# A fused LoRA matmul: the small stores ahead of one chunk's big store are cut differently and all go through GpSimd's queue

## The chip, the cores and the metric

The kernel runs on one core of a Trainium2 chip. A core has a matrix engine (TensorE, in the profile PE for matmuls and PEld for weight loads), VectorE (DVE), ScalarE (ACT), GpSimd (POOL), a queue processor (SyncE, SP) and 16 DMA engines that all queues share. Transfers issued by SP or ACT go through hardware queues; those issued by GpSimd go through a software queue, q0 in the profile. The metric is device time in microseconds of one execution.

## The reference

`x` has 16 x 2048 rows of 256 float32 numbers; `W` is 256 x 256, `lora_A` 256 x 16, `lora_B` 16 x 256, `lora_E` 16 numbers, `scale` 1.0.

```python
y = x_flat @ W
lora_out = x_flat @ lora_A
lora_out = lora_out * lora_E
lora_out = lora_out @ lora_B
y = y + scale * lora_out
```

The output is as large as `x`: 32768 rows of 1 KB, 33.55 MB in and 33.55 MB out.

## The kernel before

The low-rank part is folded into the weight once: `weff = W + A diag(E) B`, in bfloat16, so that one product per row is left.

The 32768 rows are cut into 4 chunks. A chunk is 128 partitions x 64 rows: partition p holds 64 neighbouring rows of x, 64 KB. A chunk lives in a home in SBUF, of which there are three; chunk 3 uses the home of chunk 0 again, so that its loads must wait for chunk 0's stores. The result of a row overwrites the row in its home, and is stored from there.

A chunk is worked on in 16 groups of 4 rows per partition, 64 groups in all. For each group GpSimd casts the rows to bfloat16 (line 193), TensorE transposes them (line 244), VectorE copies the transposed rows out of PSUM (line 228), TensorE multiplies (line 255), and ScalarE copies the result home (line 209). The five engines pass groups on by semaphores.

The order of the loads and stores on SP's queue is written by hand: `ORDER` at line 18. Each entry is a load ("L") or a store ("S"), a chunk and a range of its 64 rows. `sync_program` goes through it. A store waits for `s_done`, the count of finished stretches of rows; a load of chunk 3 waits for the overlapping stores of chunk 0.

Two special rules stand around the edit. First, at group (chunk 2, row 16), called `HELD`, GpSimd waits for the store of chunk 0, rows 0 to 40, to land (lines 185 to 190). Second, the first two rows of chunk 1 (`SHARED`) do not go with the big store of chunk 1, which stores rows 2 to 64. They are stored in shares of partitions: 0 to 5 and 5 to 126 by GpSimd when it gets to `HELD`, and 126 to 128 by SP just ahead of the big store (line 159). All of them wait for `s_shared`, which ScalarE raises after the first group of chunk 1 (lines 210 and 211). A transfer over many partitions is divided among the DMA engines by partition.

The program ends when SP has seen the shares land (line 162) and, in `wait_for_stores`, when `stored_rest` has counted the stores that nothing else waits for.

Of the kernel before, what the change touches and what calls it, by code (L numbers as in the profile page):

```python
# [7 lines left out]
P = 128  # L8
# [5 lines left out]
ROWS = 64  # L14
# [3 lines left out]
ORDER = [  # L18
    ("A",),
    ("L", 0, 0, 8),  # L20
    ("L", 0, 8, 24),
    ("L", 0, 24, 40),
    ("L", 0, 40, 64),
    ("L", 1, 0, 32),
    ("L", 1, 32, 64),
    ("L", 2, 0, 16),
# [2 lines left out]
    ("S", 0, 40, 64),  # L29
    ("L", 3, 0, 32),  # L30
    ("L", 3, 32, 64),
    ("S", 1, 2, 64),
    ("S", 2, 0, 64),
    ("S", 3, 0, 64),
]

SHARED = (1, 0, 2)
SHARES = ((0, 5), (5, 126))

HELD = (2, 16)  # L40
HOLDERS = (("S", 0, 0, 40),)
# [3 lines left out]
CG = 4  # L45
# [9 lines left out]
def kernel(  # L55
# [20 lines left out]
    y_chunks = out_flat.rearrange("(c p b) m -> c p b m", p=P, b=ROWS)  # L76
# [18 lines left out]
    waited = {  # L95
        op
        for op in ORDER
        if op[0] == "S" and (op in HOLDERS or op[1] < N_CHUNKS - N_HOMES)
    }
    stored = {op: sem(f"stored_{op[1]}_{op[2]}") for op in ORDER if op in waited}  # L100
    s_shared = sem("shared_done")
    shared_stored = sem("shared_stored")
    stored_rest = nc.alloc_semaphore("stored_rest")
    n_rest = 1 + sum(op[0] == "S" and op not in waited for op in ORDER)
    ends = sorted((c * ROWS + e) // CG - 1 for kind, c, s, e in (op for op in ORDER if op[0] == "S"))
    s_ident = sem("ident_made")
    s_pe_set_up = sem("pe_set_up")
# [8 lines left out]
    def home(c):  # L116
        return homes[c % N_HOMES]

    sync, gpsimd, scalar, vector, tensor = nc.sync, nc.gpsimd, nc.scalar, nc.vector, nc.tensor
# [20 lines left out]
    def sync_program():  # L140
        for n, op in enumerate(ORDER):
            if op[0] == "A":
                a = lora_A.rearrange("(q t) r -> q t r", t=KT)
                ins = sync.dma_start(out=a_sb[:], in_=a).then_inc(set_up_loaded["a"], 16)
                opening.append(ins.ins.name)
                continue
            kind, c, s, e = op
            at_home = home(c)[:, s:e, :]
            if kind == "L":
                for st in stored:  # L150
                    if st[1] == c - N_HOMES and st[2] < e and s < st[3]:
                        sync.wait_ge(stored[st], 16)
                ins = sync.dma_start(out=at_home, in_=x_chunks[c, :, s:e, :]).then_inc(loaded[op], 16)  # L153
                if n == 1:
                    opening.append(ins.ins.name)
            else:
                if c == SHARED[0]:
                    sync.wait_ge(s_shared, 1)
                    share(sync, SHARES[-1][1], P, stored_rest)
                sync.wait_ge(s_done, ends.index((c * ROWS + e) // CG - 1) + 1)  # L160
                sync.dma_start(out=y_chunks[c, :, s:e, :], in_=at_home).then_inc(stored.get(op, stored_rest), 16)
        sync.wait_ge(shared_stored, 16 * len(SHARES))

    def share(engine, first, last, landed):
        c, s, e = SHARED
        engine.dma_start(out=y_chunks[c, first:last, s:e, :], in_=home(c)[first:last, s:e, :]).then_inc(landed, 16)  # L166

    def gpsimd_program():
        gpsimd.memset(ident[:], 0.0).then_inc(s_ident, 1)  # L169
        gpsimd.wait_ge(s_ident, 1)  # L170
        gpsimd.affine_select(  # L171
            out=ident[:],
            in_=ident[:],
            compare_op=ALU.not_equal,
            fill=1.0,
            base=0,
            pattern=[[-1, P]],
            channel_multiplier=1,
        ).then_inc(s_ident, 1)
        for g in range(N_GROUPS):  # L180
            c, b = g // GPC, g % GPC * CG
            for op, landed in loaded.items():
                if op[1:3] == (c, b):
                    gpsimd.wait_ge(landed, 16)
            if (c, b) == HELD:
                gpsimd.wait_ge(s_shared, 1)
                for s, e in SHARES:
                    share(gpsimd, s, e, shared_stored)
                for op in HOLDERS:
                    gpsimd.wait_ge(stored[op], 16)  # L190
            if g >= NS:
                gpsimd.wait_ge(s_turned, g - NS + 1)
            gpsimd.tensor_copy(out=stage[g % NS][:], in_=home(c)[:, b:b + CG, :]).then_inc(s_stage[g % UNROLL], 1)  # L193

        gpsimd.wait_ge(s_turned, N_GROUPS - NS + 1)
        gpsimd.drain().then_inc(s_stage[N_GROUPS % UNROLL], 1)

    def scalar_program():
        for name, to, of in (
            ("w", w_sb, W.rearrange("(q t) m -> q t m", t=KT)),  # L200
            ("b", b_sb, lora_B),
            ("e", e_sb, lora_E[:, None]),
        ):
            ins = scalar.dma_start(out=to[:], in_=of).then_inc(set_up_loaded[name], 16)
            opening.append(ins.ins.name)
        for g in range(N_GROUPS):
            c, b = g // GPC, g % GPC * CG
            scalar.wait_ge(s_y, g + 1)
            scalar.copy(out=home(c)[:, b:b + CG, :], in_=psum_y[g % NY][:]).then_inc(s_free[(g + NY) % UNROLL], 1)  # L209
            if (c, b) == SHARED[:2]:  # L210
                scalar.drain().then_inc(s_shared, 1)
            if g in ends:
                scalar.drain().then_inc(s_done, 1)  # L213
# [76 lines left out]
    with tc.tile_critical(no_gpsimd_drain=True):  # L290
        sync_program()
        gpsimd_program()
        scalar_program()
        vector_program()
        tensor_program()
# [35 lines left out]
```

## Time and profile before

| | |
|---|---|
| median of 10 runs | 162.17 us (161.56 to 162.98) |
| the profiled execution's own time | 161.5 us |
| its span, first to last instruction | 160.2 us |
| HBM read and written | 33.85 MB and 33.55 MB, 421 GB/s over the span |
| busy: PE, DVE, ACT, POOL | 58%, 28%, 41%, 42% of the span |
| packets of SP's queue (q1) | 97.6% of the time of 16 DMA engines |
| packets of GpSimd's queue (q0) | 112 packets, 0.26 MB, 0.4% |

Everything in the profile is from one execution. A DMA engine's time is counted by packets: the share of a queue is the time its packets took, over 16 engines and the span. In views that cut a stretch into slices, a packet is counted in the slice in which it starts, so that a share can be above 1 in a short slice. TensorE's clock (PEclk) is what the throttle granted. A DMA's "us to landing" is from its issue to the last of its 16 completion signals.

### The profile page before, as it was taken

The numbers are of one execution on the slowest core, as the hardware profiler recorded it, in microseconds if no ns is written. First come the engines' busy times: TensorE is split into PE (matmuls) and PEld (weight loads), VectorE is DVE, ScalarE is ACT, GpSimd is POOL, SyncE is SP. The second block draws the span as 40 slices with busy tenths as digits, with TensorE's granted clock in tenths as the row PEclk, the third lists the DMA queues.
The fourth block names the chain that finished last, engine by engine and source line by source line (L and its number), as shares of the span: only waits on it lengthen the run. The fifth ranks groups of instructions, "written<-read, shape, count | busy, mean of one in ns | idle before, by whom it ended". The sixth has DMA issues, their size and how long they took to land.

```text
span 160.2 us, 2030 instructions
## 1 busy us (share of the span) xinstructions
PE 93.1 (58%) x782; PEld 82.0 (51%) x782; DVE 45.4 (28%) x66; ACT 66.1 (41%) x65; POOL 67.9 (42%) x72
## 2 busy tenths in 40 slices
PE   2959969959999990000999999999920000000000
PEld 1439959859999990000789999999910000000000
DVE  0245535525555550000145555555500000000000
ACT  3025775747777772000257777777740000000000
POOL 1537838387777732002567777787200000000000
PEclk9999999999999999555589999999985555555555
DMA  6999999999999997979999999989997998998993
GB/s 260 403 430 462 417 458 401 475 434 393 417 434 528 454 393 327 496 344 448 442 448 428 409 434 466 495 349 444 491 450 344 491 442 376 491 442 376 491 426 131
DMA packets 2631, 67.43 MB, mean 421 GB/s; under 512 B 496, under 2 KB 512, under 8 KB 708
## 3 DMA queue, kind: packets, MB, share of 16 engines
q1 hardware_dynamic: 2308, 66.87, 97.6%
q10 hardware_dynamic: 208, 0.28, 0.5%
q0 software_dynamic: 112, 0.26, 0.4%
q14 instruction: 3, 0.02, 0.0%
HBM read 33.85 MB, written 33.55 MB: 421 GB/s over the span
## 4 chain that ended last, share of the span: by engine, by line
DMA 43%; PE 26%; POOL 1%; ACT 1%; SPq 0%; issue 0%; ACTq 0%
DMA out_dram<-home 30%; PE psum_y L255 17%; DMA home<-in_x_dram 12%; PE psum_xt L244 9%; POOL stage L193 1%; ACT home L209 1%; SPq L153 0%; ACTq L213 0%; SPq L326 0%; SPq L290 0%
## 5 line engine op out<-in xcount | busy, mean ns | idle before, releaser
L209 ACT COPY home<-psum_y 128x1024 f32<-128x1024 f32 x64 | 64.8, 1012 | 49.9 <-PE psum_y L255 49.9
L193 POOL CAST stage<-home 128x1024 bf16<-128x1024 f32 x64 | 66.1, 1040 | 38.7 <-PE psum_xt L244 15.0
L255 PE MATMUL psum_y<-weff,xt 128*128 128x256 bf16 x512 | 68.1, 277 | 0.0
L228 DVE COPY xt<-psum_xt 128x1024 bf16<-128x1024 bf16 x64 | 44.3, 692 | 62.7 <-PE psum_xt L244 62.7
L255 PEld LDWEIGHTS psum_y<-weff,xt 128*128 128x128 bf16 x512 | 50.9, 100 | 5.8
L244 PE MATMUL psum_xt<-ident,stage 128*128 128x128 f32 x260 | 40.3, 278 | 21.0 <-POOL stage L193 20.5
L244 PEld LDWEIGHTS psum_xt<-ident,stage 128*128 128x128 f32 x260 | 31.0, 144 | 23.6 <-issue 22.2
L268 PE MATMUL psum_y<-ident 128*128 128x512 f32 x4 | 3.7, 1081 | 2.9 <-POOL ident L171 2.9
L268 PEld LDWEIGHTS psum_y<-ident 128*128 128x128 f32 x4 | 1.2, 326 | 3.9 <-POOL ident L171 2.9
L166 POOL DMA_DIRECT2D out_dram<-home x2 | 1.2, 596 | 4.6 <-DMA home<-in_x_dram 4.6
L218 DVE TENSOR_SCALAR ate<-psum_y,e_sb 16x256 f32<-16x256 f32 x1 | 0.5, 471 | 6.9 <-PE psum_y L271 6.9
L209 ACT ACT_TABLE_LOAD x1 | 1.3, 1283 | 2.1 <-SPq L290 2.1
L277 PE MATMUL psum_y<-b_sb,ate 16*128 16x256 f32 x4 | 1.1, 393 | 0.0
L169 POOL MEMSET ident<- 128x128 f32 x1 | 0.2, 204 | 1.7 <-SPq L290 1.7
L271 PEld LDWEIGHTS psum_y<-ident,a_sb 128*16 128x16 f32 x2 | 0.2, 114 | 1.2 <-issue 1.2
L232 DVE TENSOR_TENSOR weff<-w_sb,psum_y 128x512 bf16<-128x512 f32 x1 | 0.7, 689 | 0.5 <-PE psum_y L277 0.5
L277 PEld LDWEIGHTS psum_y<-b_sb,ate 16*128 16x128 f32 x4 | 0.7, 184 | 0.3 <-issue 0.2
L171 POOL TENSOR_SCALAR_AFFINE_SELECT ident<-ident 128x128 f32<-128x128 f32 x1 | 0.3, 287 | 0.2 <-POOL ident L169 0.2
L271 PE MATMUL psum_y<-ident,a_sb 128*16 128x128 f32 x2 | 0.4, 272 | 0.0
L312 POOL MEMSET const-float32-0.0<- 128x1 f32 x1 | 0.1, 98 | 0.2 <-issue 0.2
L312 POOL MEMSET const-bfloat16-1.0<- 128x1 bf16 x1 | 0.1, 101 | 0.0
L312 POOL MEMSET const-uint8-127<- 128x1 uint8 x1 | 0.1, 101 | 0.0
(1 smaller groups left out, 0.1 us busy)
## 6 DMA issues: line engine op xcount, KB each, us to landing
home<-in_x_dram SPq DMA_DIRECT2D x4, 4096.0 KB, 24.6
out_dram<-home SPq DMA_DIRECT2D x1, 7936.0 KB
home<-in_x_dram SPq DMA_DIRECT2D x3, 2048.0 KB, 13.1
home<-in_x_dram SPq DMA_DIRECT2D x1, 6144.0 KB, 57.3
out_dram<-home SPq DMA_DIRECT2D x1, 5120.0 KB, 48.4
home<-in_x_dram SPq DMA_DIRECT2D x1, 3072.0 KB, 19.9
out_dram<-home SPq DMA_DIRECT2D x1, 3072.0 KB, 46.1
home<-in_x_dram SPq DMA_DIRECT2D x1, 1024.0 KB, 5.2
```

The lines of the kernel that those rows point to most:

```text
L166: engine.dma_start(out=y_chunks[c, first:last, s:e, :], in_=home(c)[first:last, s:e, :]).then_inc(landed, 16)
L193: gpsimd.tensor_copy(out=stage[g % NS][:], in_=home(c)[:, b:b + CG, :]).then_inc(s_stage[g % UNROLL], 1)
L209: scalar.copy(out=home(c)[:, b:b + CG, :], in_=psum_y[g % NY][:]).then_inc(s_free[(g + NY) % UNROLL], 1)
L218: vector.tensor_scalar(out=ate[:], in0=psum_y[0][:R, :KT, :P], scalar1=e_sb[:], scalar2=float(scale), op0=ALU.mult, op1=ALU.mult,).then_in ...
L228: vector.tensor_copy(out=xt[g % NX][:], in_=psum_xt[g % NT][:].bitcast(BF16)).then_inc(s_xt[g % UNROLL], 1)
L232: vector.tensor_add(out=weff[:], in0=w_sb[:], in1=psum_y[1][:, :KT, :]).then_inc(s_free[0], 1)
L244: ins = tensor.transpose(psum_xt[i % NT][:, b, :], words[:, b, :], ident[:])
L255: ins = tensor.matmul(psum_y[i % NY][:, b, :], xt[i % NX][:, b, t::KT], weff[:, t, :], start=(t == 0), stop=(t == KT - 1),)
L268: tensor.matmul(psum_y[1][:, :2, :], ident[:], ident[:, None, :].to_broadcast([P, 4, P]), start=True, stop=True)
L271: ins = tensor.transpose(psum_y[0][:R, t, :P], a_sb[:, t, :], ident[:])
L277: ins = tensor.matmul(psum_y[1][:, t, :], ate[:, t, :], b_sb[:], start=True, stop=True)
L312: nc = _bacc.Bacc("TRN2", target_bir_lowering=False, num_devices=1)
```

## The change

The rows of chunk 1 that are stored apart are now its first and its last (0 and 63) instead of its first two; the big store covers rows 1 to 63. All of them go through GpSimd's queue, in four stores in this order: partitions 120 to 128 of both rows; a tiny store of 13 partitions (the first 16 numbers, 64 B, of rows 1 and 3); partitions 0 to 120 of both rows; a tiny store of 12 partitions (the first 64 B of rows 5 and 7). The tiny stores write what the big store writes again later. SP's own share is gone.

The signal `s_shared` comes after the last group of chunk 1 instead of the first. SP waits, before the big store of chunk 1, until all four have landed; in exchange the wait at the end of SP's program is gone, and the final count has one store less.

```diff
-    ("S", 1, 2, 64),
+    ("S", 1, 1, 63),
...
-SHARED = (1, 0, 2)
-SHARES = ((0, 5), (5, 126))
+SHARED = 1
+MOST = 120
...
-    n_rest = 1 + sum(op[0] == "S" and op not in waited for op in ORDER)
+    n_rest = sum(op[0] == "S" and op not in waited for op in ORDER)
...
-                if c == SHARED[0]:
-                    sync.wait_ge(s_shared, 1)
-                    share(sync, SHARES[-1][1], P, stored_rest)
+                if c == SHARED:
+                    sync.wait_ge(shared_stored, 4 * 16)
                 sync.wait_ge(s_done, ends.index((c * ROWS + e) // CG - 1) + 1)
...
-        sync.wait_ge(shared_stored, 16 * len(SHARES))
-
-    def share(engine, first, last, landed):
-        c, s, e = SHARED
-        engine.dma_start(out=y_chunks[c, first:last, s:e, :], in_=home(c)[first:last, s:e, :]).then_inc(landed, 16)
+
+    def first_and_last(p):
+        return lambda rows: rows[p, ::ROWS - 1, :]
+
+    def middles(n, b):
+        return lambda rows: rows[:n, b:b + 3:2, :16]
+
+    def share(part):
+        gpsimd.dma_start(out=part(y_chunks[SHARED]), in_=part(home(SHARED)[:])).then_inc(shared_stored, 16)
...
-                for s, e in SHARES:
-                    share(gpsimd, s, e, shared_stored)
+                for part in (first_and_last(slice(MOST, P)), middles(13, 1), first_and_last(slice(MOST)), middles(12, 5)):
+                    share(part)
...
-            if (c, b) == SHARED[:2]:
+            if (c, b + CG) == (SHARED, ROWS):
                 scalar.drain().then_inc(s_shared, 1)
```

## The prediction

> **What bounds the kernel now.** I read the table of DMA queues first, because a kernel that moves 67 MB in 160 us is most likely held by transfers; then the stretches, then the timeline around the edited lines, and last the transfers at the very end.
>
> The page of the kernel before, queue by queue (packets, MB, share of the time of 16 engines), and the two groups the edit touches:
>
> ```profile
> DMA packets 2631, 67.43 MB, mean 421 GB/s; under 512 B 496, under 2 KB 512, under 8 KB 708
> q1 hardware_dynamic: 2308, 66.87, 97.6%
> q10 hardware_dynamic: 208, 0.28, 0.5%
> q0 software_dynamic: 112, 0.26, 0.4%
> L166 POOL DMA_DIRECT2D out_dram<-home x2 | 1.2, 596 | 4.6 <-DMA home<-in_x_dram 4.6
> ```
>
> SP's queue alone fills 97.6% of sixteen DMA engines over the whole span. Its price: 0.976 x 160.2 us x 16 engines = 2502 engine-us for 66.87 MB, so 38 ns for 1 KB on one engine. GpSimd's queue (q0) carries 0.26 MB of stores, 0.4%.
>
> The same kernel in stretches (busy time of PE, PEld, DVE, ACT, POOL, then clock, DMA share, GB/s):
>
> ```profile
> 65.00:75.00 10.00, 0.00 (x0) 0.00 (x0) 0.00 (x0) 0.00 (x0) 0.00 (x0) 0.50 0.93 399
> 83.00:117.00 34.00, 34.00 (x312) 31.39 (x310) 17.29 (x25) 26.30 (x26) 24.10 (x24) 1.00 1.00 428
> 130.00:150.00 20.00, 0.00 (x0) 0.00 (x0) 0.00 (x0) 0.00 (x0) 0.00 (x0) 0.50 0.98 426
> ```
>
> The compute engines are idle for 10 us in the middle and 43 us at the end while the DMA share stays near 1. So the 26% that TensorE has in the chain of waits is no bound: the chain runs through it only because the last store is issued after the last matmul, at 118.1 us, while transfers issued before still occupy the engines. What counts is how many bytes each DMA engine carries and which engine ends last.
>
> The timeline around the edit (start us, length us, what):
>
> ```profile
> 60.26 1.01 ACT L209 COPY home<-psum_y 128x1024 f32<-128x1024 f32 x1 [0.30 <-PE psum_y L255]
> ...
> 62.40 1.18 POOL L166 DMA_DIRECT2D out_dram<-home  x2 [4.57 <-DMA home<-in_x_dram]
> 75.10 7.88 SPq L153 DMA_DIRECT2D home<-in_x_dram  x2
> 75.14 2.02 POOL L193 CAST stage<-home 128x1024 bf16<-128x1024 f32 x2 [11.56 <-DMA out_dram<-home]
> 83.03 0.34 SPq L166 DMA_DIRECT2D out_dram<-home  x1
> ```
>
> GpSimd issues its two shares at 62.4 and then waits until 75.1 for an older store. SP issues both loads of chunk 3 between 75.10 and 82.98, then its own small share at 83.03, then the big store of chunk 1. Landing times, from the list of DMA issues:
>
> ```profile
> home<-in_x_dram SPq DMA_DIRECT2D x4, 4096.0 KB, 24.6
> out_dram<-home POOLq DMA_DIRECT2D x1, 242.0 KB, 13.1
> out_dram<-home POOLq DMA_DIRECT2D x1, 10.0 KB, 7.7
> ```
>
> Last, DMA traffic from 155.5 to 157.5 us in 40 slices of 0.05 us, counted where a packet starts; one 64 KB packet in a slice reads 1311 GB/s:
>
> ```profile
> GB/s 0 0 0 0 0 0 1311 0 0 3932 0 0 5243 0 1311 0 2621 0 0 1311 0 0 1311 0 0 0 0 0 1311 0 0 0 0 0 0 1311 1311 0 0 0
> DMA packets 16, 1.05 MB, mean 524 GB/s; under 512 B 0, under 2 KB 0, under 8 KB 0
> ```
>
> These are the last 16 data packets, one on each engine. The first starts in slice 6 (155.8 us), most by 156.6, and three stragglers at about 156.9, 157.25 and 157.3. The mean is slice 16.7, 156.35 us. So the last engine is 0.95 us behind the mean, and only 0.05 us behind the next.
>
> **What the Trainium skill says.** All four places are on "DMA: Bandwidth & Descriptors". (1) "Queues, rings and completion order": an engine takes turns between queues at packet boundaries. The trace agrees: the packet records put q0's packets at about 67.4, 68.9, 70.5, 72.1 us, one for each 40 KB packet of SP's store (1.51 us). (2) "Why a DMA increments its semaphore by 16 and not by 1": a software store signals from all 16 engines whatever its shape; its engine count is the largest divisor up to 16 of the slowest dimension, on consecutive engines from a cursor that moves on, while some direct copies instead get a ceiling of partitions/16 per engine. The trace shows the second for 121 partitions: 60 packets of 4096 B and one of 2052 B, so 15 engines with 8 partitions and one with 1. The cursor is seen in no view. (3) "Latency and other measured facts": engines 7 and 15 are usually slower. No view numbers the engines. (4) "Issuing engines are not separate DMA queues": moving a transfer to another queue only saves issue time.
>
> **The change, part by part.** I count the edits to each engine's load, then each wait.
>
> *Bytes.* Before, 128 partitions x 2 KB leave ahead of the big store: 5 and 121 through GpSimd, 2 through SP. Afterwards 8 and 120 through GpSimd. The big store stays 62 rows. Added: 25 tiny stores' partitions x 2 x 64 B = 3.2 KB. So the mean load over engines is unchanged; only its distribution moves.
>
> *Light engine.* Before, one engine carries 2 KB where others carry 16 or 18: it is spared 14 KB x 38 ns = 0.54 us. Afterwards one engine again has no part of the 120, by either rule of the skill. By the cursor rule, starting at engine c: 8 on c to c+7, 13 on c+8 to c+20, so 15 start at c+5 and leave out c+4; the 12 close the circle (8+13+15+12 = 48). Then c+4 keeps one partition of the eight and is spared 0.54 us relative to the plain ones, and seven carry one extra partition, 0.08 us (before: five and two, the same number). By the ceiling rule the spared engine is the last, as before. The effect is a swap of the spared engine.
>
> What does a swap bring? If the engine newly spared is the last, the end moves only to the next straggler, 0.05 us; if it is any of the 13 others, nothing. The one losing the relief: following packets end to start, one engine moves about 0.6 us ahead of the others between 61 and 75 us, which I take for the one with one partition, and its last packet begins at 156.3. Put 0.54 later it begins at 156.84, still 0.45 before the last. So from -0.05 to 0 here; I take 0.
>
> *Run length.* The two rows are no longer neighbours, so each partition sends two runs of 1 KB in place of one of 2 KB. Lowest cost zero, if four runs share a 4 KB packet as two do now. Highest: by q10, which holds the 1 to 2 KB packets: 0.5% x 2563 engine-us / 0.28 MB = 47 ns per KB against 38, 9 ns x 256 KB / 16 = 0.14 us per engine. I take 0.02. Two more semaphore writes per engine and one or two tiny packets: packets of 4 B and 128 B take 9 and 12 ns in the records, together about 0.04 us.
>
> *GpSimd's queue.* Two more issues at about 0.6 us: 1.2 us, from 63.6 to 64.8; scaled by descriptors (240 runs against 121) perhaps 65.6. The wait to 75.08 hides it with about 10 us to spare; uncovered it would cost those 1 to 2 us of staging. The signal it waits for now comes from the last group of chunk 1 rather than the first; ACT's copy at 60.26 is group 34, so group 31 ended near 57.3, before GpSimd arrives at 62.1. Cost 0.
>
> *SP's queue.* One issue (0.34 us) and a late wait disappear. Added: SP waits for all four stores before the big store of chunk 1. Behind it stand the stores of chunks 2 and 3. Landing: per engine 7 turns before (data, signal, four data, signal), from 67.4 to 75.7; afterwards up to 11. Five at 1.52 us reach 75, six at the 0.91 us of the next store's 24 KB packets reach 80.5. SP is busy with loads until 82.98, so no wait. If every 1 KB run were its own packet, 23 turns: five, eight to 82.3, ten beside 32 KB loads at 1.21 us: about 94. Even then the queue holds the loads of chunk 3: the second, issued just before 82.98, needs about 20 us, to 102. Cost 0 as long as landing is before about 99.
>
> *Sum.* Against the profiled execution of 161.5 us (span 160.2, 1.3 around it): 0.02 + 0.04 + 0 = +0.06, so 161.56. This execution was 0.67 below the median of 162.17; added there: 162.2.
>
> **Rivals.** (A) As summed, the swap and small costs below what a measurement tells: 162.2, between 161.75 and 162.6. For it: full queues, unchanged bytes, the two late stragglers so close together. Against: one execution's ranking of engines may be chance.
>
> (B) The newly spared engine is the one that ends last in most executions, and the second straggler of this profile is usually absent. Then the gain is the gap to the third, 0.4, to the full relief, 0.54: 161.65. For it: long before the end the stragglers were struck by 8 KB instruction fetches (queue q14, 67.6, 86.4 and 101.5 us in the records), which may hit the same engines each time. Against: at least three engines are hit, and one is spared.
>
> (C) Slower: the engine that loses its 0.54 us becomes the last. In the profile it lacks 0.45; from the point where it runs more than that later it decides, and a run where it was already at the straggler's place would lose the 0.54 plus 0.08 for a second partition: 162.8. For it: the skill's slow engine 15 and the fact that in the records this engine is the latest of all at 61 us, 0.25 behind the mean. Against: the 0.45.
>
> (D) Landing after about 99 us: the queue runs dry and each us late costs one. It needs twice the turns of my worst count; at 102 it gives 165.
>
> That the spared engine stays the same (ceiling rule) is within A: 162.2.
>
> **How the numbers follow.** A 0.57, B 0.20, C 0.17, D 0.06. Anything within 0.3%, 0.49 us, can't be told from no change for this kernel, whose ten times spread over 1.4 us. B lies at 0.52, just outside: faster 0.19, rest to same; C and D give slower 0.23; same 0.58. The range holds A, most of B and C: 161.45 to 163.0. Outside it are D and the far ends of B and C.
>
> **What would show it.** Right: q1 loses its two 2 KB packets and q0 grows by 50 to 90 packets; GpSimd's issues end by 66 us; SP's big store is issued near 83.1; the last 16 packets have the same mean within 0.1 us. Wrong: a DMA share below 0.9 near 100 us (D); an engine ending alone at the back with the others ahead (C); the last two stragglers gone (B).

## The result, and the profile after

The changed kernel takes 162.87 us (median of 15 runs, 162.3 to 163.56), the kernel before 161.99 us (53 runs, 161.35 to 162.98) on the same chips. The ratio is 1.0052, with a 95% interval of 1.0037 to 1.0068: slower by about 0.85 us. The forecast was 162.2 with no measurable difference as the likeliest; the time lies inside the stated range, on the side that had 0.23.

The profiled execution took 163.17 us, span 161.8; that of before took 161.5, span 160.2. This pair is 1.6 us apart, twice the medians, so the sizes below are larger than the typical effect.

The page of the changed kernel, queues and the software stores:

```profile
DMA packets 2691, 67.43 MB, mean 417 GB/s; under 512 B 556, under 2 KB 572, under 8 KB 768
q1 hardware_dynamic: 2304, 66.86, 97.2%
q0 software_dynamic: 176, 0.27, 0.4%
L169 POOL DMA_DIRECT2D out_dram<-home x4 | 2.6, 648 | 4.4 <-DMA home<-in_x_dram 4.4
```

The bytes are the same, q0 has 64 packets more, and SP's queue still fills the engines: 97.2% of 161.8 us is 157.3 us of packets on each engine, against 97.6% of 160.2, 156.4, before. So 0.9 of the 1.6 us are packets that took longer for the same bytes; the other 0.7 belong to one engine that ends late, as the last packets below show. The same three stretches as before:

```profile
65.00:75.00 10.00, 0.00 (x0) 0.00 (x0) 0.00 (x0) 0.00 (x0) 0.30 (x2) 0.50 0.93 398
83.00:117.00 34.00, 32.71 (x299) 30.01 (x297) 16.73 (x25) 24.88 (x26) 23.17 (x23) 1.00 1.03 433
130.00:150.00 20.00, 0.00 (x0) 0.00 (x0) 0.00 (x0) 0.00 (x0) 0.00 (x0) 0.50 1.04 452
```

TensorE, never idle from 83 to 117 us before, now is for 1.3 us. The timeline around the edit:

```profile
60.49 1.01 ACT L212 COPY home<-psum_y 128x1024 f32<-128x1024 f32 x1 [0.30 <-PE psum_y L258]
62.48 2.58 POOL L169 DMA_DIRECT2D out_dram<-home  x4 [4.41 <-DMA home<-in_x_dram]
74.71 8.53 SPq L153 DMA_DIRECT2D home<-in_x_dram  x2
74.75 2.02 POOL L196 CAST stage<-home 128x1024 bf16<-128x1024 f32 x2 [9.70 <-DMA out_dram<-home]
...
83.35 0.36 SPq L160 DMA_DIRECT2D out_dram<-home  x1
```

Nothing is late here. GpSimd's four issues end at 65.06, its wait at 74.75 (before: 75.14). SP's big store is issued at 83.35 (before: 83.42). The landings, from the list of DMA issues:

```profile
out_dram<-home POOLq DMA_DIRECT2D x1, 240.0 KB, 14.1
...
out_dram<-home POOLq DMA_DIRECT2D x1, 16.0 KB, 7.8
out_dram<-home POOLq DMA_DIRECT2D x1, 1.6 KB, 9.8
out_dram<-home POOLq DMA_DIRECT2D x1, 1.5 KB, 15.2
```

The last tiny store, issued at 64.49, lands at 79.7. The loss shows where the traffic turns round. Two short stretches, first of the kernel before, then of the changed one (busy times, clock, DMA share, GB/s). Near 81 us the engines go over from the second store of chunk 0 to the loads of chunk 3, near 101 us from these loads to the big store of chunk 1:

```profile
79.50:82.50 3.00, 3.00 (x21) 2.43 (x20) 1.08 (x2) 1.50 (x2) 1.40 (x2) 0.67 1.02 431
98.50:102.50 4.00, 4.00 (x39) 3.73 (x38) 2.10 (x4) 3.04 (x3) 3.19 (x4) 1.00 1.18 478
```

```profile
79.50:82.50 3.00, 3.00 (x28) 2.69 (x27) 1.45 (x3) 1.79 (x3) 2.12 (x3) 0.94 1.10 429
98.50:102.50 4.00, 4.00 (x39) 3.71 (x38) 2.08 (x3) 3.11 (x4) 3.12 (x3) 1.00 1.25 446
```

Divide GB/s by DMA share to see what the engines moved for their busy time: 431/1.02 = 423 before and 390 after in the first, 405 and 357 in the second. GpSimd then meets a wait that the kernel before did not have, on the last load of chunk 3. The timeline of GpSimd, before and after:

```profile
101.79 1.04 POOL L193 CAST stage<-home 128x1024 bf16<-128x1024 f32 x1 [0.27 <-PE psum_xt L244]
103.17 1.04 POOL L193 CAST stage<-home 128x1024 bf16<-128x1024 f32 x1 [0.34 <-PE psum_xt L244]
```

```profile
101.38 1.04 POOL L196 CAST stage<-home 128x1024 bf16<-128x1024 f32 x1 [0.27 <-PE psum_xt L247]
104.53 2.02 POOL L196 CAST stage<-home 128x1024 bf16<-128x1024 f32 x2 [2.11 <-DMA home<-in_x_dram]
```

And the end of the changed kernel's data, in slices of 0.05 us from 156.5 to 158.5 us:

```profile
GB/s 0 1311 0 1311 1311 0 1311 0 0 2621 1311 3932 0 0 0 2621 0 0 0 1311 1311 0 0 0 0 0 1311 0 0 0 0 0 0 0 0 1311 0 0 0 0
```

Sixteen packets start here. Fifteen are the last of their engines; one, at 156.66 by the packet records, is the last but one of the sixteenth engine, whose last starts at 159.07. So two things moved: the mean start of the last packets, from 156.35 to 157.32 us, and the straggler, from 0.97 to 1.75 us behind the mean.

To follow this in every run I use one sum from the packet records, called **turn loss** below. Number SP's large packets in the order of their starts, 16 to a round, one round for each time that all engines take a packet. Between the mean start of the last 24 KB round of the store and the first 32 KB round of the load, a packet at its usual pace needs 0.912 us; between the starts of the load's last round but one and of the big store's first round, two need 2.426 us. What the two distances have above that is the turn loss. It comes from the one profiled execution of each kernel. Where an engine is more than a packet behind, neighbouring rounds mix; followed engine by engine, from packet end to packet start, the sums differ by up to 0.1 us. Before: 0.06 + 0.29 = 0.35 us. After: 0.28 + 0.97 = 1.25 us. The difference, 0.90, is nearly all of the 0.97 that the mean end moved. From the first packet of chunk 0's first store to the last of its second, the stretch in which GpSimd's stores travel, it grew only from 19.10 to 19.16. At the second turn the longest load packet of each engine took 1.22 to 1.99 us before and 1.56 to 2.40 after, where 1.21 is the usual.

The straggler is made at the second turn too. In the changed kernel's records the latest engine is 0.74 us behind the mean in the last but one load, and 1.8 behind when its big store begins; before, the latest was 0.75 and then 1.05 behind. On that engine one load packet took 2.40 us, and a fetch of instructions 0.79 us just after it. This is a single execution, and the medians are only 0.88 us apart.

### The profile page after: what moved, and what is told of

It is laid out like the page before. It is cut to its first block, busy times and chain, and to the rows that moved or that the text cites. A ratio compares the mean times of both kernels' runs of the same rounds, so it can differ in the third digit from the quotient of the medians.

```text
span 161.8 us, 2031 instructions
## 1 busy us (share of the span) xinstructions
PE 93.5 (58%) x782; PEld 81.9 (51%) x782; DVE 45.4 (28%) x66; ACT 66.1 (41%) x65; POOL 69.1 (43%) x74
## 3 DMA queue, kind: packets, MB, share of 16 engines
q1 hardware_dynamic: 2304, 66.86, 97.2%
## 4 chain that ended last, share of the span: by engine, by line
DMA 60%; PE 8%; POOL 1%; ACT 1%; SPq 1%; issue 1%; ACTq 0%
DMA home<-in_x_dram 32%; DMA out_dram<-home 29%; PE psum_y L258 5%; PE psum_xt L247 3%; POOL stage L196 1%; ACT home L212 1%; SPq L153 1%; ACTq L216 0%; SPq L329 0%; SPq L152 0%; SPq L293 0%
## 5 line engine op out<-in xcount | busy, mean ns | idle before, releaser
L212 ACT COPY home<-psum_y 128x1024 f32<-128x1024 f32 x64 | 64.8, 1012 | 50.6 <-PE psum_y L258 50.6
L247 PE MATMUL psum_xt<-ident,stage 128*128 128x128 f32 x260 | 40.9, 281 | 21.3 <-POOL stage L196 20.9
L169 POOL DMA_DIRECT2D out_dram<-home x4 | 2.6, 648 | 4.4 <-DMA home<-in_x_dram 4.4
```

Of the source, the lines that this page charges most:

```text
L169: gpsimd.dma_start(out=part(y_chunks[SHARED]), in_=part(home(SHARED)[:])).then_inc(shared_stored, 16)
L247: ins = tensor.transpose(psum_xt[i % NT][:, b, :], words[:, b, :], ident[:])
```

## The experiments

Each measured ratio is against the kernel before, timed on the same chip. In the edits "..." stands between places of the kernel that lie apart; the counts that a wait or the end of the program expects go along with them. Three theories were held at first: P, the engine that lost its relief ends last; N (in later runs R), what is stored (rows 0 and 63, two 1 KB runs, the big store from row 1); W, the wait and the later signal.

**No engine spared.** One GpSimd store of all 128 partitions, SP's share dropped.

```diff
-SHARES = ((0, 5), (5, 126))
+SHARES = ((0, 128),)
...
-                    share(sync, SHARES[-1][1], P, stored_rest)
```

> The kernel before with all 128 partitions of rows 0 and 1 of chunk 1 in one GpSimd store, and SP's share gone: every DMA engine gets 16 KB, none is spared. Theory P (place): the 0.9 us come from the engine that lost its relief, which then ends last; the spared engine of the changed kernel was not a late one. Then this kernel is as slow as the changed one: 162.7 to 163.1. Theory N (near packets): it comes from what is stored (rows 0 and 63, 1 KB runs, the big store beginning at row 1): then 162.0 to 162.2. Theory W (wait and signal): 162.0 to 162.2 too.

Measured 161.57 us, ratio 0.9971 (0.9951 to 0.9990), turn loss 0.06. All three theories missed: taking the relief away altogether, with one store in place of three, made the kernel faster. So relief lost is not what the change pays for, and P falls.

**The four stores on neighbouring rows.** The changed kernel with rows 0 and 1.

```diff
-    ("S", 1, 1, 63),
+    ("S", 1, 2, 64),
...
-        return lambda rows: rows[p, ::ROWS - 1, :]
+        return lambda rows: rows[p, :2, :]
...
-        return lambda rows: rows[:n, b:b + 3:2, :16]
+        return lambda rows: rows[:n, b + 1:b + 4:2, :16]
```

> The changed kernel with rows 0 and 1 in place of 0 and 63, the big store from row 2, the tiny stores moved into rows 2 to 9; four stores and the wait as changed. Theory N: back to 162.0. Theory W: stays at 162.9. Theory P: depends on the rule that divides 120 partitions of neighbouring rows: if the last engine is spared as for the 121 before, 162.0; if the place follows the cursor, 162.9. The packets of q0 show which: by the cursor rule 8 stores' packets of 2048 B and an engine with empty packets of 16 B, as in the changed kernel.

Measured 162.35 us, ratio 1.0033 (1.0014 to 1.0052), turn loss 1.08. The changed kernel has four packets of 16 B in q0, this one none, so the division differs, as under the ceiling rule. It does not go back to the time of before although 120 partitions are divided by that rule, and its interval overlaps that of the changed kernel: against N, though a part for the rows is not excluded here.

**Another engine spared.** Tiny stores of 8, 9 and 8 partitions.

```diff
-                    sync.wait_ge(shared_stored, 4 * 16)
+                    sync.wait_ge(shared_stored, 5 * 16)
...
-                for part in (first_and_last(slice(MOST, P)), middles(13, 1), first_and_last(slice(MOST)), middles(12, 5)):
+                for part in (first_and_last(slice(MOST, P)), middles(8, 1), first_and_last(slice(MOST)), middles(9, 5), middles(8, 9)):
```

> The changed kernel with the tiny stores on 8, then 9 and 8 partitions in place of 13 and 12 (five stores, the wait counts five): by the cursor rule the spared engine is c+15 instead of c+4, and the partition of the first eight no longer falls on it. Theory P: if c is 0 this spares engine 15, as before, and the time goes back to 162.0, or 0.1 to 0.2 above for one more store; if c is something else, any value between 162.0 and 162.9. Theories N and W: 162.9.

Measured 163.36 us, ratio 1.0071 (1.0041 to 1.0102), turn loss 1.23. The place did move: in the records, followed from packet end to packet start, the light engine of the changed kernel has one of the eight 2 KB packets, here it has none. Moving the spared engine did not bring the time back. With five stores it is no faster than with four.

**The wait and the signal alone**, in the kernel before.

```diff
-                    sync.wait_ge(s_shared, 1)
+                    sync.wait_ge(shared_stored, 16 * len(SHARES))
                     share(sync, SHARES[-1][1], P, stored_rest)
...
-        sync.wait_ge(shared_stored, 16 * len(SHARES))
...
-            if (c, b) == SHARED[:2]:
+            if (c, b + CG) == (SHARED[0], ROWS):
```

> The kernel before with the changed signal (after the last group of chunk 1) and with SP's wait for GpSimd's shares ahead of its own share instead of at the end. Theory W: 162.6 to 163. Theories P and N: 162.0, since the shares land near 76 us and SP gets there at 83.

Measured 161.85 us, ratio 0.9994 (0.9975 to 1.0014), turn loss 0.27. W falls.

The times now stood in the order of the number of software stores: one, two, four, five. That was a new theory, C, and four runs tested it.

**No software store at all.** Rows 0 and 1 go with the big store; GpSimd's shares, SP's share and their signals are gone.

```diff
-    ("S", 1, 2, 64),
+    ("S", 1, 0, 64),
...
-                for s, e in SHARES:
-                    share(gpsimd, s, e, shared_stored)
...
-                    share(sync, SHARES[-1][1], P, stored_rest)
```

> The kernel before without any store through GpSimd: the big store of chunk 1 takes all 64 rows, rows 0 and 1 go with it. Theory C (count: each store through the software queue costs some 0.3 us, read off one store 161.57, two 161.91, four 162.35 to 162.87, five 163.36): 161.2 to 161.4. Theory P (relief of one engine is worth something): at or above the kernel with the even store, 161.6 to 162. Theory R (what is stored, not how often): 161.5 to 161.7, as with one even store.

Measured 161.66 us, ratio 0.9972 (0.9953 to 0.9992), turn loss 0.07. The ratio is that of one even store: against a cost for each store, at least from none to one.

**One even store of rows 0 and 63.**

```diff
-                    sync.wait_ge(shared_stored, 4 * 16)
+                    sync.wait_ge(shared_stored, 16)
...
-                for part in (first_and_last(slice(MOST, P)), middles(13, 1), first_and_last(slice(MOST)), middles(12, 5)):
+                for part in (first_and_last(slice(P)),):
```

> One GpSimd store of rows 0 and 63 over all 128 partitions (two 1 KB runs each, even load), the wait and signal as changed, no tiny stores. Theory C: as the one even store of rows 0 and 1, 161.5 to 161.7. Theory R (1 KB runs, or the big store from row 1): 162.0 to 162.3, since the step from the adjacent version to the changed kernel was 0.5.

Measured 161.51 us, ratio 0.9959 (0.9941 to 0.9976), turn loss 0.21: the rows, the 1 KB runs and the big store from row 1 cost nothing. N falls for good. The two stretches of this kernel, which read as those of before or better (437/1.02 = 428 and 485/1.17 = 415 GB/s of busy time):

```profile
79.50:82.50 3.00, 3.00 (x24) 2.67 (x23) 1.20 (x2) 1.96 (x2) 1.52 (x2) 0.79 1.02 437
98.50:102.50 4.00, 4.00 (x39) 3.73 (x38) 2.08 (x3) 3.04 (x3) 3.19 (x4) 1.00 1.17 485
```

**Two tiny stores added** to the kernel with the moved wait.

```diff
                 for s, e in SHARES:
                     share(gpsimd, s, e, shared_stored)
+                for n, b0 in ((13, 3), (12, 7)):
+                    tiny(n, b0)
...
```

> The kernel before with the moved wait and two tiny stores (13 and 12 partitions, 64 B of two rows each) behind GpSimd's two shares: four software stores, the load of the engines as before. Theory C: 162.3 to 162.6. Theories P and R: 161.9, as the kernel with the moved wait.

Measured 162.43 us beside 162.21 for before, ratio 1.0013 (0.9989 to 1.0037), turn loss 0.67. Inconclusive: between the two forecasts as a ratio. The profiled execution, from which the turn loss is, took 163.4, near the slowest of its 22.

**The tiny stores dropped** from the changed kernel.

```diff
-                for part in (first_and_last(slice(MOST, P)), middles(13, 1), first_and_last(slice(MOST)), middles(12, 5)):
+                for part in (first_and_last(slice(MOST, P)), first_and_last(slice(MOST))):
...
```

> The changed kernel without its tiny stores: 8 and 120 partitions of rows 0 and 63, two software stores, and by the cursor rule another engine spared in each execution. Theory C: 161.9 to 162.1. Theory R: 162.3 to 162.9. Theory P: a wide spread between executions, 162 to 163.3, since some spare a late engine and others do not.

Measured 162.49 us, ratio 1.0027 (1.0007 to 1.0047), turn loss 1.00. The times spread from 161.77 to 163.45, as P forecast, but those of the kernel before spread as far on this chip (161.3 to 163.48), so this tells nothing. Two stores as before, yet slower than before: the count of software stores is not all. Next to the one even store (0.9959) what differs is that there are two, and how they are divided. Hence theory S: unequal shares put the engines out of step, and this is paid where the traffic turns. The last four runs set S against C.

**Four stores, real ones even.**

```diff
-... first_and_last(slice(MOST, P)), middles(13, 1), first_and_last(slice(MOST)), middles(12, 5) ...
+... first_and_last(slice(64, P)), middles(13, 1), first_and_last(slice(64)), middles(12, 5) ...
```

> The changed kernel with the two real stores cut at 64 and 64 partitions instead of 8 and 120: still four software stores in the same order with the same tiny ones and the same wait, but each engine gets 4 partitions from each, none is spared. Theory S (one engine spared runs ahead, and the others pay where the traffic turns from stores to loads and back): as the one even store, 161.4 to 161.7. Theory C (each software store costs): 162.1 to 162.5.

Measured 162.55 us, ratio 1.0069 (1.0040 to 1.0098), turn loss 0.86. S as it was put missed: no engine is spared the 14 KB (in the records every engine has four packets of 4096 B), and it is as slow as the changed kernel. What stays uneven are 13 and 12 packets of 128 B. The second stretch moves 471/1.24 = 380 GB/s of busy time:

```profile
98.50:102.50 4.00, 4.00 (x40) 3.72 (x38) 2.08 (x3) 3.11 (x4) 3.12 (x3) 1.00 1.24 471
```

**One software store, one engine spared.** 120 partitions through GpSimd, 8 by SP.

```diff
                     sync.wait_ge(shared_stored, 16)
+                    part = first_and_last(slice(MOST, P))
+                    sync.dma_start(out=part(y_chunks[c]), in_=part(home(c)[:])).then_inc(stored_rest, 16)
...
-                for part in (first_and_last(slice(P)),):
+                for part in (first_and_last(slice(MOST)),):
```

> One software store, of 120 partitions of rows 0 and 63 over 15 engines, and the other 8 partitions by SP just ahead of the big store: one engine spared, no tiny store. Theory S: 162.2 to 162.6, as the version with 8 and 120 and no tiny stores. Theory C: 161.5 to 161.7, as the one even store.

Measured 162.26 us, ratio 1.0032 (1.0007 to 1.0056), turn loss 0.88. Now C missed: with a single software store still, the 0.4% gain of the even store became a 0.3% loss. But two things changed: one engine is spared, and SP has a small store of its own directly ahead of the big store, which is where the second turn lies (471/1.26 = 374):

```profile
98.50:102.50 4.00, 4.00 (x39) 3.72 (x38) 2.15 (x4) 3.11 (x4) 3.20 (x4) 1.00 1.26 471
```

**The relief doubled.** Four rows in the kernel before's three shares.

```diff
-    ("S", 1, 2, 64),
+    ("S", 1, 4, 64),
...
-SHARED = (1, 0, 2)
+SHARED = (1, 0, 4)
```

> The kernel before with four rows in the shares instead of two (5, 121 and 2 partitions as before; the big store from row 4): the engine that is spared is spared 28 KB instead of 14 KB, about 1.1 us instead of 0.54. Theory S: 0.3 to 0.8 above the kernel before, 162.3 to 162.9. Theory C: 162.0, the number of stores is the same.

Measured 163.17 us, ratio 1.0085 (1.0062 to 1.0109), turn loss 1.18: as S had it, slower by more than it forecast, with the number and the queues of the stores unchanged.

**The control**, the same four rows in one even store (the edit above on the kernel with no engine spared).

> The same four rows in one even store of 128 partitions through GpSimd: the control for the version with four rows in three shares. Theories S and C: 161.5 to 161.8, as with two rows, if the amount that goes through the software queue costs nothing by itself; above 162 if it does.

Measured 161.55 us, ratio 0.9983 (0.9967 to 1.0000), turn loss 0.07. With two rows, uneven against even is 0.0029 of the time; with four it is 1.0085 - 0.9983 = 0.0102. Twice the bytes in the software queue cost about a tenth of a per cent when they are one even store, which is within the intervals, and 0.85% when they go in uneven shares.

All runs by what GpSimd's stores do:

| kernel | software stores | all of them on 16 engines evenly | turn loss, us | ratio |
|---|---|---|---|---|
| none | 0 | yes | 0.07 | 0.9972 |
| one even, rows 0 and 1 | 1 | yes | 0.06 | 0.9971 |
| one even, rows 0 and 63 | 1 | yes | 0.21 | 0.9959 |
| one even, four rows | 1 | yes | 0.07 | 0.9983 |
| before | 2 | no | 0.35 | 1 |
| before, wait moved | 2 | no | 0.27 | 0.9994 |
| before, two tiny added | 4 | no | 0.67 | 1.0013 |
| 8 and 120, no tiny | 2 | no | 1.00 | 1.0027 |
| 120 alone | 1 | no | 0.88 | 1.0032 |
| four stores, rows 0 and 1 | 4 | no | 1.08 | 1.0033 |
| changed kernel | 4 | no | 1.25 | 1.0052 |
| four stores, 64 and 64 | 4 | tiny ones not | 0.86 | 1.0069 |
| five stores | 5 | no | 1.23 | 1.0071 |
| before, four rows | 2 | no | 1.18 | 1.0085 |

What is shown: the loss goes with how the small stores are cut, not with the rows, the run length or the wait, and about 0.9 us of the profiled difference lie at the two turns. The four kernels whose software stores are even, or absent, are the four fastest, with turn losses up to 0.21; all others lie at 0.27 and above, though the next one, before with the wait moved, is within the intervals of the fourth.

What is not shown is which property of the cut it is. The four fast kernels are also the only ones with at most one small store, counting those of SP's queue as well (120 alone has two). No run varies the division alone between one store and several. For the division speaks that twice the bytes in the same three uneven shares cost 0.85%. Against it speaks that the 64 and 64 kernel, with the same four stores as the changed one but the real ones even, gained nothing; only packets of 128 B, 12 ns each, were uneven there. Several even software stores without tiny ones were not tried, nor an even store beside a small one of SP, so a cost of every small store beyond the first stays open as a rival. Uneven shares and tiny stores are not seen to add: the changed kernel has both, and its interval overlaps those of the kernels with one of them.

Nor is it shown how the loss comes about at the turns. Engines out of step, so that some read HBM while others still write, would fit the even controls, but the records speak against it. In the 64 and 64 kernel the engines stand closer together before the first turn (latest 0.23 us behind the mean) than with one even store of rows 0 and 63 (0.46), and it still loses 0.19 there. Before the second turn, in the last but one load, the sixteen starts spread alike in the changed kernel and in the one even store of four rows (standard deviation 0.35 us in both), and the losses there are 0.97 and 0.05.

One version beats both kernels: the single even store of rows 0 and 63, 161.51 us, 0.9959 of before. Leaving the software stores out altogether is as good within the intervals.

## Why the prediction was right or wrong

- **The bound** was right: SP's queue at 97% of the engines, compute hidden.
- **SP's queue, cost 0**: right. The big store is issued at 83.35, the last small store has landed at 79.7 (80.5 forecast), and the wait alone measured 0.9994.
- **GpSimd's queue, cost 0**: right. 2.58 us for four issues, done at 65.06 (64.8 to 65.6 forecast), with 9.7 us of the old wait left.
- **Run length, 0.02 us**: right in size. The records have 60 packets of 4096 B at 159 ns for the 120 partitions, as before, so four runs share a packet; the one even store of rows 0 and 63 is not slower than that of rows 0 and 1.
- **Small packets and signals, 0.04 us**: right where they travel. The stretch from the first packet of chunk 0's first store to its last grew by 0.06 us, which is the sum that was forecast for the whole.
- **The light engine, taken as 0**: the step that failed. It added bytes for each engine by itself, and let the end move only if another engine became the last. The forecast that the last packets keep their mean within 0.1 us was wrong by 0.9: packets were lengthened at two turns of the traffic, on about ten engines at the first and on all sixteen at the second, 20 us after the small stores had landed. The sum had no term for that. In its place the profiles put a turn loss of 0.35 us in the kernel before and 1.25 in the changed one; why there is such a loss stays open.
- **The time inside the range is luck** as far as the sum goes: it came to +0.06 us, the medians are 0.88 apart. The width that the rivals gave the range took it in.
- **The sign of relief.** The prediction held that sparing an engine 14 KB could only help it or do nothing. Dropping the relief, and with it two of the three shares, gained 0.29%; doubling it cost 0.85%.
- **Rival C**, the slower one, had the right side and nearly the right time (162.8) by the wrong mechanism: there is a straggler, but the mean of all engines moved by 0.97 us too, and a kernel without any relief is faster. D did not occur. B's gain by sparing a late engine was not seen in the two places of the spared engine that were tried.

## What to carry to other kernels

When the DMA engines are the bound, add up not only bytes for each engine: look at the packets on both sides of every change between stores and loads, and compare GB/s over DMA share there with the same stretch of another version. Among large transfers, try small stores as one transfer divided evenly over all 16 engines, or leave them in the large one: these were the fastest versions here, without it being known whether the evenness or the single transfer did it. A trick that relieves one engine is to be timed against plainly even work, not only against another relief.

## What the runs showed that was not expected

- Small stores cut differently go with longer packets 20 us later: between one even store and 120 partitions with SP's share of 8, the mean end of all sixteen engines moved by 0.6 us (158.80 to 159.37 by the packet records), though the work that was moved is 14 KB on one engine, 0.54 us of its time.
- In the profiles one engine runs slower during the big store of chunk 1, which runs beside compute: its 62 KB packets take about 2.49 us instead of 2.34, one after another, about 1 us in all, and its packets are back at full speed in the next store. Which engine it is shows in no view, and why it is slower stays open.
- A fetch of instructions is an 8 KB packet on a data engine, three in the span, of 0.31 us each but for the one of 0.79 in the changed kernel. The fetch near 86 us is followed on its engine by a load packet 0.53 us longer than usual. In the profiles of the kernel before and of the changed one, the two fetches after 80 us fell on engines that were among the last to end.
